# Score blocks of 32 keys written to their own partitions in a chunkwise scan

## The chip, the cores and the metric

The kernel runs on one core of a Trainium2 chip. The metric is the device time of one execution in microseconds (us); lower is better. All inputs and outputs are float32.

## The reference, cut to what matters

One layer of a diffusion trunk: an adaLN-modulated RMSNorm, an HGRN2 gated linear recurrence in both directions over 256 context and 2048 latent tokens with 8 heads of 128 channels, a projection, and then a gated ConvFFN. The change touches the recurrence alone. Per head and direction it is computed in chunks:

```python
b = jnp.cumsum(logf, axis=3)
b_ref = b[:, :, :, CHUNK // 2:CHUNK // 2 + 1]
b_last = b[:, :, :, -1:]
qe = q * jnp.exp(b - b_ref)
ke = k * jnp.exp(b_ref - b)
scores = jnp.einsum('bhnik,bhnjk->bhnij', qe, ke)
...
scores = jnp.where(mask, scores, 0.0)          # key not later than query
o_intra = jnp.einsum('bhnij,bhnjv->bhniv', scores, v)
kv = jnp.einsum('bhnjk,bhnjv->bhnkv', k * jnp.exp(b_last - b), v)
# state: s = decay * s + kv, chunk after chunk
o_inter = jnp.einsum('bhnik,bhnkv->bhniv', q * jnp.exp(b), s_start)
o = o_intra + o_inter
```

The result of the two directions is added, so for a pair of tokens there is one score: from the forward direction where the key is not later than the query, from the backward direction where it is not earlier (both on the diagonal).

## The kernel before, in words

The kernel has a mixer stage (the scan, up to about 1327 us of the profile), an output projection and a ConvFFN. Only the scan is changed. It walks over two groups of token tiles (`GROUPS`, line 39), in each over 8 heads, and in each over units of three tiles of 128 tokens (`unit`, line 362). For a unit, TensorE computes the gates of both directions, q and the values by products split into three passes (`mm3`, line 353; lines 356 to 358 are the bulk of its work). VectorE then makes cumulative products inside segments of 32 tokens (`S`, `F`, twelve segments in a unit), the keys `ke` and queries `qp` scaled within a segment, and from them by further factors `kd`, `qe`, `qi`, `qm`, `km` (`scaled`, line 489). `rt` holds the reciprocal of a segment's whole decay, `TB` and `TX` hold products of the segments' decays, made on GpSimd.

The steps of a tile are two closures. `part_a` (line 538) transposes `kd`, forms the tile's scores, merges them under masks into a 128 x 128 matrix `at` (keys on partitions, queries in columns). `part_b` (line 569) forms the state's update `kv`, the output `o` from the state and from `at`, and sends the results to a stash in DRAM. The closures of one unit are not run at once: `unit` returns them in an `order` list, and the next unit runs them between its own products (`fill`, `tick`), so that TensorE always has the big products to go on with. A scheduler below the program may move an instruction within its engine's queue.

The scores of a tile before: four products of 128 keys by 128 queries into one PSUM tile `sc` (lines 550, 551, 556, 557), of which each only fills a part that is used. `sc[:, 0]` and `sc[:, 1]` hold the forward and backward scores inside segments of 32 (with `qe`), `sc[:, 2]` those between the two segments of a 64-token pair (with the key copies `kx`), and `sc[:, 3]` those between the two pairs (`km`, `qm`). ScalarE copies two 64 x 64 corners of `sc[:, 3]` into the buffer `af` (lines 561 and 562), VectorE copies the rest under three masks (lines 563 to 565) and adds the two buffers (line 566).

A float32 product appears in the trace as two passes, each with its weight load (LDWEIGHTS) and its MATMUL. The program's one other place with products of fewer output rows than 128 within the scan is `ada_rest` (line 628): sums over partitions with a weight of one column.

Of the kernel before, what the change touches and what calls it, by code (L numbers as in the profile page):

```python
# [9 lines left out]
F32 = mybir.dt.float32  # L10
F32R = mybir.dt.float32r
BF16 = mybir.dt.bfloat16
U32 = mybir.dt.uint32
AF = mybir.ActivationFunctionType
OP = mybir.AluOpType
# [29 lines left out]
NS = 12  # L45
# [3 lines left out]
def body(ctx, tc, a, out):  # L49
    nc = tc.nc  # L50
    pe, act, dve, pool, sp = nc.tensor, nc.scalar, nc.vector, nc.gpsimd, nc.sync
# [38 lines left out]
    def pool_(stack, name, bufs=1, **kw):  # L90
        return stack.enter_context(tc.tile_pool(name=name, bufs=bufs, reuse_waits="tile", **kw))
# [94 lines left out]
    with ExitStack() as c0:  # L186
# [15 lines left out]
        first = [t for u in GROUPS[0] for t in u]  # L202
        for k in range(KT):
            for i in range(2):
# [3 lines left out]
                for n in range(2):  # L208
                    pe.matmul(mps[2 * i + n], silv[:, k, :], wt[:, n * 512:(n + 1) * 512],
                              start=k == 0, stop=k == KT - 1)  # L210
# [16 lines left out]
        for g in range(2):  # L227
            ks = slice(g * 4, g * 4 + 4)
            for j, hm in enumerate(hms):
                m = 0 if first[j] >= 0 else 1  # L230
# [9 lines left out]
        mx = p0.tile([128, 16], F32, name="mx")  # L240
# [38 lines left out]
    def mixer_scan():  # L279
        gp = pool_(c1, "gp", side="right")  # L280
        xp = pool_(c1, "xp", side="right")
        ps = pool_(c1, "ps", space=PSUM)
# [3 lines left out]
        def in_block(m, blk):  # L286
            n = 128 // blk
            pool.affine_select(out=m, in_=m, pattern=[[-blk, n], [0, blk]],
                               compare_op=OP.is_ge, fill=0.0, base=0, channel_multiplier=1)
            pool.affine_select(out=m, in_=m, pattern=[[blk, n], [0, blk]],  # L290
                               compare_op=OP.is_ge, fill=0.0, base=blk - 1, channel_multiplier=-1)

        def mask(name):
            m = fix.tile([128, 4, 32], F32, name=name)
            pool.memset(m, 1.0)
            return m

        mf, mb, mx = mask("mf"), mask("mb"), mask("mx")
        in_block(mb, 32)
        in_block(mx.rearrange("p (a c) b -> p a (c b)", c=2), 64)  # L300
        dve.tensor_tensor(mx, mx, mb, OP.subtract)
        in_block(mf, 32)
        for m, s in ((mf, 1), (mb, -1)):

            pool.affine_select(out=m, in_=m, pattern=[[32 * s, 4], [s, 32]],
                               compare_op=OP.is_ge, fill=0.0, base=0, channel_multiplier=-s)
        mfu, mbu, mxu = [m.rearrange("p a b -> p (a b)").bitcast(U32) for m in (mf, mb, mx)]
        d1 = fix.tile([128, NS, SEG], BF16, name="d1")
        pool.memset(d1, 0.0)
        pool.memset(d1[:, :, 0:1], 1.0)  # L310
# [11 lines left out]
        count = {"F": 0, "A": 0}  # L322
# [39 lines left out]
        def unit(h, w, u, tiles, todo, fine=False):  # L362
# [5 lines left out]
            g0 = 4 * s0  # L368
            lat = slice(g0, NS)
# [28 lines left out]
            for d in range(2):  # L398
# [4 lines left out]
                j = (1 - d) * NH + h  # L403
# [23 lines left out]
            q = gp.tile([128, nq], F32, name="q", tag="q", bufs=2)  # L427
# [24 lines left out]
            ke = gp.tile([128, 2, NS, 32], F32, name="ke", tag="ke", bufs=2)  # L452
# [9 lines left out]
            rt = gp.tile([128, 2, NS], F32, name="rt", tag="rt", bufs=2)  # L462
            dve.reciprocal(rt[:, :, lat], S[:, :, lat, 32])

            qp = gp.tile([128, 2, NS, 32], F32, name="qp", tag="qp", bufs=2)
# [23 lines left out]
            def scaled(dst, src, w):  # L489

                w = w[..., None].to_broadcast(list(w.shape) + [32])
                dve.tensor_tensor(dst, src, w, OP.mult)
# [7 lines left out]
            scaled(kd, ke, TBf[:, 0:4:3])  # L500


            qe = gp.tile([128, 2, NS, 32], F32, name="qe", tag="qe", bufs=2)
            scaled(qe[:, :, lat], qp[:, :, lat], rt[:, :, lat])
            qi = gp.tile([128, 2, NS, 32], F32, name="qi", tag="qi", bufs=2)
            scaled(qi[:, :, lat], qp[:, :, lat], TBf[:, 1:3, lat])

# [1 line left out]
            qm = gp.tile([128, NSC, 4, 32], F32, name="qm", tag="qm", bufs=2)  # L509
            km = gp.tile([128, NSC, 4, 32], F32, name="km", tag="km", bufs=2)  # L510
# [2 lines left out]
            scaled(km[:, s0:, 0:2], seg(ke[:, 1])[:, :, 0:2], TX[:, 1, s0:, 0:2])  # L513
            scaled(km[:, s0:, 2:4], seg(ke[:, 0])[:, :, 2:4], TX[:, 1, s0:, 2:4])

            kx = gp.tile([128, NS, 32], F32, name="kx", tag="kx", bufs=2)
            act.activation(kx[:, g0::2], ke[:, 1, g0::2], AF.Copy)
            act.activation(kx[:, g0 + 1::2], ke[:, 0, g0 + 1::2], AF.Copy)

            if s0:  # L520
                z = ps.tile([128, s0, 128], F32, name="z", tag="pj", bufs=3)
# [16 lines left out]
            def part_a(s):  # L538
                g4 = slice(4 * s, 4 * s + 4)
                tr = ps.tile([128, 2, 128], F32, name="tr", tag="tr")  # L540
                for d in range(2):
                    pe.transpose(tr[:, d], kd[:, d, g4], ident)
                kt = gp.tile([128, 2, 128], F32, name="kt", tag="kt", bufs=3)
                act.activation(kt, tr, AF.Copy)
                kts[s] = kt
                if s < s0:
                    return

                sc = ps.tile([128, 4, 128], F32, name="sc", tag="sc", bufs=2)
                pe.matmul(sc[:, 0], ke[:, 0, g4], qe[:, 0, g4], start=True, stop=True)  # L550
                pe.matmul(sc[:, 1], ke[:, 1, g4], qe[:, 1, g4], start=True, stop=True)

                c0 = qp[:, 0, 4 * s]
                qx = bass.AP(tensor=c0.tensor, offset=c0.offset,
                             ap=[list(c0.ap[0]), [64, 2], [(NS + 1) * 32, 2], [1, 32]])
                pe.matmul(sc[:, 2], kx[:, g4], qx, start=True, stop=True)
                pe.matmul(sc[:, 3], km[:, s], qm[:, s], start=True, stop=True)
                at = gp.tile([128, 128], F32, name="at", tag="at", bufs=2)
                af, ab = ABs[count["A"] % 2]
                count["A"] += 1  # L560
                act.activation(af[0:64, 64:128], sc[0:64, 3, 64:128], AF.Copy)
                act.activation(af[64:128, 0:64], sc[64:128, 3, 0:64], AF.Copy)
                dve.copy_predicated(af, mxu, sc[:, 2])
                dve.copy_predicated(af, mbu, sc[:, 0])
                dve.copy_predicated(ab, mfu, sc[:, 1])
                dve.tensor_tensor(at, af, ab, OP.add)
                ats[s] = at

            def part_b(s):
# [33 lines left out]
                sp.dma_start(stash[t][:, 0, h, 1], qi[:, 0, g4].rearrange("p g t -> p (g t)"))  # L603

            order = ((part_a, 0), (part_a, 1), (part_b, 0), (part_a, 2), (part_b, 1), (part_b, 2))
            return [lambda f=f, s=s: f(s) for f, s in order]

# [47 lines left out]
        for g, units in enumerate(GROUPS):  # L655
            for h in range(NH):
                if g == h == 0:
                    w = head0
                else:
                    w = load_feat(h)  # L660
                    load_vg(h, w)
                for u, tiles in enumerate(units):
                    todo, fine = list(unit(h, w, u, tiles, todo, fine)), False
                    if h > 0 and steps < 16 * (g + 1):
                        next(rest, None)
                        steps += 1
                    if g == h == u == 0:
                        todo, fine = with_h(todo, [m[-2:] for m in third], [None] * 3), True
                        todo = [m[0] for m in third[1:]] + todo
                    if g == 0 and h == NH - 2 and u == 2:  # L670
                        todo += [m[0] for m in new[0:2]]
                    if g == 0 and h == NH - 1:
                        loads = [m[0] for m in new[3 * u + 2:3 * u + 5]]
                        todo = with_h(todo, [m[1:] for m in new[3 * u:3 * u + 3]],
                                      loads + [None] * (3 - len(loads)))
                        fine = True
                    if g == 1 and h == NH - 1:
                        if u == 0:
                            todo.append(gate1)
                        for j, k in enumerate(range(3 * u, min(3 * u + 3, KT))):  # L680
                            todo.insert(len(todo) if u < 2 else j,
                                        lambda k=k: out_weight(k))
        for f in todo:
            f()

    mixer_scan()
    c1.close()

# [63 lines left out]
    qp = pool_(fq, "qp", side="right")  # L752
# [70 lines left out]
    first = [Pair(1, q) for q in range(2)]  # L823
# [225 lines left out]
    ps = pool_(fp, "psa", 2, space=PSUM)  # L1049
# [200 lines left out]
    ps = pool_(fb, "psb", 8, space=PSUM)  # L1250
# [169 lines left out]
    for s in range(N):  # L1420
        ph, c = divmod(s, NC)
# [84 lines left out]
```

## Time and profile before

| | us |
|---|---|
| median of 3 runs | 2856.59 (2854.42 to 2858.09) |
| span of the profiled execution | 2852.8 |
| TensorE (PE) busy in it | 2803.9 |
| its weight loads (PEld) | 2503.4 |
| VectorE (DVE) busy | 2080.8 |
| ScalarE (ACT) busy | 1176.5 |
| GpSimd (POOL) busy | 570.1 |

The span runs from the first to the last instruction of the profiled execution; the median of the runs is 3.8 us above it. Groups of instructions are shown as: line, engine, operation, output<-inputs, shapes, count | busy us in total, mean ns of one | idle time of the engine before them and what ended it. Rows of the timeline start with the start in us and the duration in us, and end with the number of instructions merged. In rows of one line's instructions the three numbers are the smallest, median and longest duration in ns, and 128*32 would mean 128 rows and 32 columns of the TensorE array. Matmuls overlap and their ends are modelled, so the distance of their starts is what they cost.

### The profile page before, as it was taken

Reading aid. Unit: us, or ns where it says so; the run is one execution under the profiler, and the core shown is the slowest. Engines: PE = TensorE matmul, PEld = TensorE weight load, DVE = VectorE, ACT = ScalarE, POOL = GpSimd, SP = SyncE. Lnnn points to the kernel's source line nnn. Section 1 sums busy time; section 2 is a strip of 40 time slices with the busy share of each in tenths; the row PEclk is TensorE's granted clock in tenths of the full one; section 3 lists DMA queues with packets and bytes.
Section 4 is the critical chain, followed back from the end, with each engine's and each line's share of the span. In section 5 each row is a group of like instructions: output and inputs, shape, how many; then the busy total and the mean of one; then the engine's idle time right before and its main releaser. Section 6 shows DMA issues by size and latency. Waiting matters only on the chain. (4 is left out here: it accounts for less than half of the span.)

```text
span 2852.8 us, 43739 instructions
## 1 busy us (share of the span) xinstructions
PE 2803.9 (98%) x16016; PEld 2503.4 (88%) x16016; DVE 2080.8 (73%) x3698; ACT 1176.5 (41%) x2517; POOL 570.1 (20%) x1020
## 2 busy tenths in 40 slices
PE   7999999999999999998999899999999999999999
PEld 4999999999999999998888688888888888887887
DVE  5766666677667566587898787777887777676887
ACT  5433333355333323333555444444444444333343
POOL 2111111121111111111111243433443342000001
PEclk9999999999999999999999999999999999999999
DMA  6222222222232222135778622225522223987663
GB/s 237 67 79 79 84 76 84 79 78 89 85 90 66 80 78 85 61 98 185 266 293 315 227 86 71 88 82 190 187 89 89 76 73 115 310 301 252 194 200 122
DMA packets 202623, 385.51 MB, mean 135 GB/s; under 512 B 26660, under 2 KB 117796, under 8 KB 197160
## 3 DMA queue, kind: packets, MB, share of 16 engines
q1 hardware_dynamic: 199672, 374.46, 39.1%
q10 hardware_dynamic: 2736, 8.26, 0.8%
q8 instruction: 126, 2.06, 0.3%
q14 instruction: 89, 0.73, 0.1%
HBM read 280.65 MB, written 101.99 MB: 134 GB/s over the span
## 5 line engine op out<-in xcount | busy, mean ns | idle before, releaser
L356 PE MATMUL z<-vh,hh 128*128 128x256 f32 (+1 forms) x1024 | 300.3, 293 | 0.0
L358 PE MATMUL z<-vh,hl 128*128 128x256 f32 (+1 forms) x1024 | 293.4, 287 | 0.0
L357 PE MATMUL z<-vl,hh 128*128 128x256 f32 (+1 forms) x1024 | 293.3, 286 | 0.0
L356 PE MATMUL z<-hh,wh 128*128 128x384 f32 x768 | 264.1, 344 | 0.7 <-ACT hh L80 0.7
L357 PE MATMUL z<-hl,wh 128*128 128x384 f32 x768 | 258.4, 336 | 0.5 <-DVE hl L81 0.5
L358 PE MATMUL z<-hh,wl 128*128 128x384 f32 x768 | 258.7, 337 | 0.0
L1338 PE MATMUL y<-wd,ml 128*128 128x512 f32 x600 | 234.0, 390 | 2.1 <-DVE ml L81 2.1
L1336 PE MATMUL y<-wd,mh 128*128 128x512 f32 x600 | 233.8, 390 | 0.9 <-DVE P L1390 0.7
L1337 PE MATMUL y<-wd,mh 128*128 128x512 f32 x600 | 233.5, 389 | 0.0
L356 PEld LDWEIGHTS z<-vh,hh 128*128 128x128 f32 x1024 | 196.3, 192 | 0.0
L357 PEld LDWEIGHTS z<-vl,hh 128*128 128x128 f32 x1024 | 196.1, 191 | 0.0
L358 PEld LDWEIGHTS z<-vh,hl 128*128 128x128 f32 x1024 | 195.8, 191 | 0.0
L81 DVE TENSOR_TENSOR w<-raw,w 128x512 fp32r<-128x512 f32 x180 | 141.9, 793 | 43.1 <-ACT w L80 41.1
L484 POOL COPY TX<-S 128x3 f32<-128x3 f32 x48 | 14.6, 304 | 792.4 <-DVE S L448 792.4
L80 ACT ACTIVATE w<-raw 128x512 fp32r<-128x512 f32 x180 | 111.8, 629 | 141.2 <-PE zd L741 78.6
L81 DVE TENSOR_TENSOR w<-s,w 128x512 fp32r<-128x512 f32 x126 | 122.3, 976 | 49.4 <-ACT w L80 48.6
L424 DVE TENSOR_TENSOR st<-z,st 128x128 f32<-128x128 f32 x127 | 36.5, 287 | 158.7 <-ACT st L423 158.6
L356 PEld LDWEIGHTS z<-hh,wh 128*128 128x128 f32 x768 | 145.3, 189 | 4.4 <-DVE acc L620 1.7
L419 ACT ACTIVATE v<-z 128x128 f32<-128x128 f32 x128 | 35.4, 277 | 271.1 <-PE z L358 271.1
L357 PEld LDWEIGHTS z<-hl,wh 128*128 128x128 f32 x768 | 145.2, 189 | 0.7 <-DVE hl L81 0.7
L358 PEld LDWEIGHTS z<-hh,wl 128*128 128x128 f32 x768 | 144.7, 188 | 0.0
L738 PE MATMUL zc<-rT,w 128*128 128x512 f32 x352 | 137.1, 389 | 2.7 <-ACT w L80 2.7
(337 smaller groups left out, 8119.8 us busy)
## 6 DMA issues: line engine op xcount, KB each, us to landing
raw<-in_w_up_dram SPq DMA_DIRECT2D x88, 512.0 KB, 3.8
raw<-in_w_in_dram SPq DMA_DIRECT2D x80, 512.0 KB, 3.7
lr<-m SPq DMA_DIRECT2D x49, 512.0 KB, 5.5
m<-r SPq DMA_DIRECT2D x66, 256.0 KB, 4.3
raw<-in_w_ada_dram SPq DMA_DIRECT2D x32, 512.0 KB, 4.5
stash<-st SPq DMA_DIRECT2D x125, 128.0 KB, 1.9
kq<-stash SPq DMA_DIRECT2D x15, 1024.0 KB, 7.4
og<-stash SPq DMA_DIRECT2D x15, 1024.0 KB, 6.3
```

The costliest lines, as they stand in the source:

```text
L80: act.activation(h, src, AF.Copy)
L81: dve.tensor_tensor(l, src, h.bitcast(F32), OP.subtract)
L356: pe.matmul(o, sh[:, k], mh[:, k], start=k == 0, stop=False)
L357: pe.matmul(o, sh[:, k], ml[:, k], start=False, stop=False)
L358: pe.matmul(o, sl[:, k], mh[:, k], start=False, stop=k == KT - 1)
L419: act.activation(v[:, s], z[:, 0:128], AF.Copy)
L424: dve.tensor_tensor(st[:, 1], z[:, 128:256], st[:, 1], OP.mult)
L484: pool.tensor_copy(TX[:, 0, :, 0], tot[:, 0, :, 1])
L738: pe.matmul(o, w[:, 0, k], r[:, :, 0, k], start=start and k == 0, stop=False, skip_group_check=True)
L1336: pe.matmul(z, lh, rh, start=start, stop=False, skip_group_check=True)
L1337: pe.matmul(z, lh, rl, start=False, stop=False, skip_group_check=True)
L1338: pe.matmul(z, ll, rh, start=False, stop=stop, skip_group_check=True)
```

## The change

Scores are formed in blocks of 32 keys, each written to the 32 partitions of its own keys: twelve products a tile, eight of them with 64 query columns and four with 32. The factor that carries a pair of 32-token segments over its inner border is multiplied in place, once, into the first or second segment's queries and keys (`halves`), so the scores of a whole 64-token pair of one direction come from one scaling; `qe` and `kx` go. The two PSUM tiles `scs` are made once, set to zero, and taken in turn, since blocks that no product writes are read under the mask. The masks now cover pairs of 64; the scores between the two pairs are written beside the forward ones in `sc[:, 0]` and come along with its masked copy, so the two copies on ScalarE and one masked copy on VectorE go.

```diff
-        mf, mb, mx = mask("mf"), mask("mb"), mask("mx")
-        in_block(mb, 32)
-        in_block(mx.rearrange("p (a c) b -> p a (c b)", c=2), 64)
-        dve.tensor_tensor(mx, mx, mb, OP.subtract)
-        in_block(mf, 32)
+        mf, mb = mask("mf"), mask("mb")
+        for m in (mf, mb):
+            in_block(m.rearrange("p (a c) b -> p a (c b)", c=2), 64)
         for m, s in ((mf, 1), (mb, -1)):
             pool.affine_select(out=m, in_=m, pattern=[[32 * s, 4], [s, 32]],
                                compare_op=OP.is_ge, fill=0.0, base=0, channel_multiplier=-s)
-        mfu, mbu, mxu = [m.rearrange("p a b -> p (a b)").bitcast(U32) for m in (mf, mb, mx)]
+        for i in range(2):
+            pool.memset(mb[64 * i:64 * i + 64, 2 - 2 * i:4 - 2 * i], 1.0)
+        mfu, mbu = [m.rearrange("p a b -> p (a b)").bitcast(U32) for m in (mf, mb)]
+        scs = [ps.tile([128, 2, 128], F32, name=f"sc{i}", tag=f"sc{i}", bufs=1) for i in range(2)]
+        for sc in scs:
+            dve.memset(sc, 0.0)
...
-            qe = gp.tile([128, 2, NS, 32], F32, name="qe", tag="qe", bufs=2)
-            scaled(qe[:, :, lat], qp[:, :, lat], rt[:, :, lat])
...
-            kx = gp.tile([128, NS, 32], F32, name="kx", tag="kx", bufs=2)
-            act.activation(kx[:, g0::2], ke[:, 1, g0::2], AF.Copy)
-            act.activation(kx[:, g0 + 1::2], ke[:, 0, g0 + 1::2], AF.Copy)
+            def halves(x, first):
+                c = x[:, 0, g0 + first]
+                step, inner = (32, [1, 32]) if len(x.shape) > 3 else (1, [0, 32])
+                return bass.AP(tensor=c.tensor, offset=c.offset,
+                               ap=[list(c.ap[0]), [(NS + 1 - 2 * first) * step, 2],
+                                   [2 * step, (NS - g0) // 2], inner])
+
+            for x, first in ((qp, 1), (ke, 0)):
+                dve.tensor_tensor(halves(x, first), halves(x, first), halves(rt, first), OP.mult)
...
-                sc = ps.tile([128, 4, 128], F32, name="sc", tag="sc", bufs=2)
-                pe.matmul(sc[:, 0], ke[:, 0, g4], qe[:, 0, g4], start=True, stop=True)
-                pe.matmul(sc[:, 1], ke[:, 1, g4], qe[:, 1, g4], start=True, stop=True)
-
-                c0 = qp[:, 0, 4 * s]
-                qx = bass.AP(tensor=c0.tensor, offset=c0.offset,
-                             ap=[list(c0.ap[0]), [64, 2], [(NS + 1) * 32, 2], [1, 32]])
-                pe.matmul(sc[:, 2], kx[:, g4], qx, start=True, stop=True)
-                pe.matmul(sc[:, 3], km[:, s], qm[:, s], start=True, stop=True)
+                sc = scs[count["A"] % 2]
+
+                def score(d, k, kc, q, qc):
+                    pe.matmul(sc[32 * kc.start:32 * kc.stop, d, 32 * qc.start:32 * qc.stop],
+                              k, q, start=True, stop=True, skip_group_check=True)
+
+                for j in range(4):
+                    kc, qc = slice(j, j + 1), slice(2 - j // 2 * 2, 4 - j // 2 * 2)
+                    score(0, km[:, s, kc], kc, qm[:, s, qc], qc)
+                for d in range(2):
+                    for j in range(4):
+                        kc = slice(j, j + 1)
+                        qc = slice(j // 2 * 2, j // 2 * 2 + 2) if j % 2 == 1 - d else kc
+                        score(d, ke[:, d, 4 * s + j], kc,
+                              qp[:, d, 4 * s + qc.start:4 * s + qc.stop], qc)
                 at = gp.tile([128, 128], F32, name="at", tag="at", bufs=2)
                 af, ab = ABs[count["A"] % 2]
                 count["A"] += 1
-                act.activation(af[0:64, 64:128], sc[0:64, 3, 64:128], AF.Copy)
-                act.activation(af[64:128, 0:64], sc[64:128, 3, 0:64], AF.Copy)
-                dve.copy_predicated(af, mxu, sc[:, 2])
                 dve.copy_predicated(af, mbu, sc[:, 0])
                 dve.copy_predicated(ab, mfu, sc[:, 1])
                 dve.tensor_tensor(at, af, ab, OP.add)
```

## The prediction

> **What bounds the kernel now.** I began with the page: the busy shares, and the strips in 40 slices.
>
> ```profile
> span 2852.8 us, 43739 instructions
> PE 2803.9 (98%) x16016; PEld 2503.4 (88%) x16016; DVE 2080.8 (73%) x3698; ACT 1176.5 (41%) x2517; POOL 570.1 (20%) x1020
> PE   7999999999999999998999899999999999999999
> PEclk9999999999999999999999999999999999999999
> ```
>
> TensorE is busy in nearly all slices, at the full granted clock; VectorE has a quarter of the span free and ScalarE more than half. An average of this kind does not settle one stage, so I asked next for the busy time in stretches of the scan, where all scores lie (their lines run from 86 to 1324 us), and for TensorE's own waits up to 1340 us.
>
> ```profile
> 300.00:700.00 400.00, 396.47 (x2809) 388.72 (x2808) 272.05 (x626) 169.54 (x478) 69.94 (x198) 1.00 0.27 84
> 700.00:1000.00 300.00, 300.00 (x2176) 297.08 (x2176) 195.88 (x434) 99.50 (x307) 38.74 (x126) 1.00 0.26 80
> ```
>
> ```profile
> PE kv L574 <- DVE Sf L593: 2.9, 5, 0.7
> ...
> PE sc L550 <- DVE AB L565: 0.3, 1, 0.3
> ```
>
> In the columns (stretch, then busy time of PE, its weight loads, DVE, ACT, POOL) PE is busy for 300.00 of 300.00 us while DVE is busy for 195.88 and ACT for 99.50. The longest wait of PE for DVE inside the scan sums to 2.9 us; that of the scores is 0.3 us. So in the scan time is TensorE time: what the change adds to PE's stream is paid in full, and what it takes from DVE and ACT is paid back only in those few waits.
>
> **What the change takes from DVE and ACT.** These are the groups it removes (a line, busy total, mean ns):
>
> ```profile
> L492 DVE TENSOR_TENSOR qe<-qp,rt 128x768 f32<-128x768 f32 (+1 forms) x48 | 41.3, 860 | 0.0
> L563 DVE COPY_PREDICATED AB<-mx,sc 128x128 f32<-128x128 uint32 x128 | 36.8, 290 | 2.3 <-ACT AB L562 2.3
> L562 ACT ACTIVATE AB<-sc 64x64 f32<-64x64 f32 x128 | 28.1, 220 | 2.6 <-issue 0.2
> L561 ACT ACTIVATE AB<-sc 64x64 f32<-64x64 f32 x128 | 27.5, 215 | 32.6 <-PE sc L557 32.5
> L517 ACT ACTIVATE kx<-ke 128x192 f32<-128x192 f32 (+1 forms) x48 | 16.6, 346 | 70.6 <-DVE ke L454 70.6
> L518 ACT ACTIVATE kx<-ke 128x192 f32<-128x192 f32 (+1 forms) x48 | 16.4, 342 | 53.9 <-DVE ke L453 53.8
> L453 DVE TENSOR_TENSOR ke<-S 128x384 f32<-128x384 f32 x48 | 26.8, 559 | 0.3
> ```
>
> ACT loses 28.1 + 27.5 + 16.6 + 16.4 = 88.6 us. DVE loses 41.3 + 36.8 = 78.1 us and gains two multiplications per unit of at most 384 columns, half of them from qp and half from ke; by the row of ke (L453, as many columns, 0.559 us) that is 48 × 2 × 0.559 = 54 us, so DVE ends 24 us lighter. All of it lies beside a busy PE. I put its worth at nothing, between 0 and the 3.2 us of the two waits above, which it could shorten; the set-up (two memsets of PSUM, other masks) runs once, on engines that PE does not wait for there, and I put it at nothing too.
>
> The new multiplications stand at the end of DVE's preparation of a unit, and the scores wait for them. Their cover is this stretch, where DVE ends a unit's last product (qm) and PE reaches that unit's first transposes:
>
> ```profile
> 708.59 0.35 DVE L492 TENSOR_TENSOR qm<-qp,TX 128x192 f32<-128x192 f32 x1
> ...
> 718.32 0.38 PE L542 MATMUL tr<-ident,kd 128*128 128x128 f32 x2
> ```
>
> That is 718.32 − 708.94 = 9.4 us of slack for 1.1 us of work, while qe's 0.9 us ahead of it goes. Queued behind it on DVE are the st products of the same unit, which read PE's z buffers and so free them, three in turn; they come 1.1 − 0.9 = 0.2 us later.
>
> **What it does to TensorE: the streaming.** Before, a tile has four score products, and each is two passes (256 instructions for 128 tiles):
>
> ```profile
> L550 PE MATMUL sc<-qe,ke 128*128 128x128 f32 x256 | 49.6, 275 | 0.3 <-DVE AB L565 0.3
> L556 PE MATMUL sc<-qp,kx 128*128 128x128 f32 x256 | 49.5, 275 | 0.0
> ```
>
> The mean of 275 ns is latency, since matmuls overlap. The cost is the distance between starts, read from the timeline (start, duration, line; two passes each):
>
> ```profile
> 702.83 0.39 PE L550 MATMUL sc<-qe,ke 128*128 128x128 f32 x2
> 703.06 0.39 PE L551 MATMUL sc<-qe,ke 128*128 128x128 f32 x2
> 703.28 0.39 PE L556 MATMUL sc<-qp,kx 128*128 128x128 f32 x2
> 703.50 0.39 PE L557 MATMUL sc<-qm,km 128*128 128x128 f32 x2
> 703.73 0.61 PE L574 MATMUL kv<-v,kt 128*128 128x128 f32 x4
> ```
>
> From 702.83 to 703.73 is 0.90 us for eight passes, 0.111 us a pass of 128 columns, and 0.89 us a tile. After, a tile has twelve products of 32 keys: eight with 64 query columns and four with 32. That is 16 passes of 64 and 8 of 32 columns, 1280 columns streamed in place of 1024, in 24 passes in place of 8.
>
> What such a short pass costs is not in this trace; three bounds are. If passes go in file at the same rate per column, it is 16 × 0.0555 + 8 × 0.0278 = 1.11 us a tile. If the four groups of 32 output partitions work side by side without loss, it is a quarter, 0.28 us. The upper bound is the shortest matmuls of this trace, sixteen transposes with two moving columns at the start:
>
> ```profile
> 34.98 0.90 PE L220 MATMUL mt<-ident,m 2*128 2x2 f32 x12
> ...
> L220 PE MATMUL mt<-ident,m x16: 195/196/218, 35.0 to 36.7; 2*128 2x2 f32 x16
> ```
>
> Twelve of them start over 0.90 − 0.196 = 0.70 us, 0.064 us from one weight load and matmul to the next though almost nothing streams; 24 of those are 1.54 us. I take a value between: the two passes of one call add into the same partitions and go in file, and a call into other partitions starts while the last pass of the call before still streams, half of that 0.064 us behind it. A call is then one pass and a start: 0.0555 + 0.032 = 0.088 us with 64 columns, 0.028 + 0.032 = 0.060 us with 32. The tile is 8 × 0.088 + 4 × 0.060 = 0.94 us, 0.05 us more than now, or 6 us over 128 tiles. It is nearest to the file (1.11 us), whose rate is the only one seen in a stream of products.
>
> The Trainium skill (TensorEngine Tiling (Array Packing), Instruction Overhead) speaks against cutting a dimension that is already small: a matmul has about 60 cycles of overhead, so one column takes as long as sixty. The 0.064 us of L220 says the same and more. By the page's figure at 2.4 GHz, 25 ns a pass, the 24 passes could not take under an estimated 0.60 us, and with 0.60 us for the 0.94 us above the sum below would come out near 2860 us.
>
> **The switch of the array.** The new products use 32 of the array's columns, everything around them 128. This trace shows what such a change costs at one place, the sums with a weight of one column (L628), between products of 128:
>
> ```profile
> 319.64 0.28 PE L357 MATMUL z<-vl,hh 128*128 128x256 f32 x1
> 319.76 0.28 PE L358 MATMUL z<-vh,hl 128*128 128x256 f32 x1
> 319.97 1.88 PE L628 MATMUL z<-acc,ones 128*1 128x512 f32 x4
> 321.77 0.44 PE L356 MATMUL z<-hh,wh 128*128 128x384 f32 x1
> 322.06 0.34 PE L357 MATMUL z<-hl,wh 128*128 128x384 f32 x1
> 322.23 0.34 PE L358 MATMUL z<-hh,wl 128*128 128x384 f32 x1
> ```
>
> ```profile
> L628 PEld LDWEIGHTS z<-acc,ones x16: 79/82/83, 320.0 to 1179.6; 128*1 128x1 f32 x16
> L628 PE MATMUL z<-acc,ones x16: 590/592/593, 320.0 to 1180.0; 128*1 128x512 f32 x16
> ...
> L550 PEld LDWEIGHTS sc<-qe,ke x256: 186/190/192, 86.4 to 1323.3; 128*128 128x128 f32 x128
> ```
>
> Going in: L358 follows L357 by 0.12 us, but L628 follows L358 by 0.21, so 0.09 us is lost. Going out: the four passes of L628 start (1.88 − 0.59) / 3 = 0.43 us apart, so the last ends its stream at 319.97 + 4 × 0.43 = 321.69. The following product should start there. The one after it starts at 322.06, and at the usual distance of 0.17 us (322.23 − 322.06) the first really started at 321.89: 0.20 us lost, as if the array ran empty and then waited for a whole weight load. Together 0.29 us for each excursion. A first load of 32 columns instead of one adds by the two load rows (190 − 82) / 127 × 31 = 26 ns. So 0.32 us a tile, 41 us in all, if every tile makes one excursion; in this timeline the scores of a tile stand together, between transposes and the kv products. It is zero if what L628 shows belongs to its own operands, and twice that if the order puts other products between a tile's twelve.
>
> **The sum.** 128 × (0.94 − 0.89 + 0.32) = 47 us on the profiled span of 2852.8 us, that is 2900 us; the median of the runs lies 3.8 us above that span, so 2904 us. About 0.2% (6 us) is what a measurement of this kernel can tell from no change.
>
> **The rivals.**
>
> *The groups really work side by side (faster).* With the switches at 0.32 us, the change gains as soon as a tile's 24 passes take less than 0.89 − 0.32 = 0.57 us. Full overlap, 0.28 us, gives 128 × (0.28 + 0.32 − 0.89) = −37 us, 2819 us; midway between 0.57 and 0.28, 0.43 us, it is 2838 us. For it: the blocks go to different partitions, and PE already lays weight loads beside matmuls. Against it: L220's 0.064 us, nearly nine times the 0.28 / 24 = 0.012 us that full overlap needs. The Trainium skill (TensorE: Matmul & The Clock Gate, Part 3) has column tiles running at once and reports 2.38 times the speed for three of them at 512 columns. By that figure the file's 1.11 us would be an estimated 0.47 us and the kernel some 13 us faster; no run here shows such short passes.
>
> *In file.* 1.11 us a tile: 128 × (1.11 + 0.32 − 0.89) = 69 us, 2926 us. For it: in the rows above no matmul starts closer to the one before than that one streams.
>
> *A floor for each load and matmul.* 24 × 0.064 = 1.54 us: 128 × (1.54 + 0.32 − 0.89) = 124 us, 2981 us. For it: L220. Against: its weights have 128 columns, these 32.
>
> *A wait in place of the removed copies.* If the in-place multiplications come so late that each unit's first scores wait out their 1.1 us, 48 × 1.1 = 53 us come on top of the sum, 2957 us. The slack of 9.4 us speaks against it.
>
> *The switches are not there, or cancel.* Without them 0.94 us gives 2863 us and 0.89 us gives no change.
>
> **How the numbers follow.** The forecast case has 0.37, in file 0.21, the floor 0.14, the late multiplications 0.05. Side by side has 0.17, all of it counted as faster; no switches or a cancellation within 0.2% has 0.06, of which 0.05 count as the same. Faster 0.17, same 0.05, slower 0.78. The range of 2838 to 2982 us takes in the floor and the weaker half of side by side.
>
> **What would show it.** In the changed profile the score line should have 3072 matmuls in place of 1024, its passes in other partitions some 0.03 us behind each other, and the distance from the last transpose to the first score and from the last score to the next product should be 0.1 and 0.2 us longer than the streams. DVE should be about 24 us and ACT about 89 us lighter, with PE as full as now and no new wait of PE for DVE. I am wrong if a tile's scores, switches included, take under 0.89 us, or if PE waits for ke or qp.

## The result and the profile after

The changed kernel takes 2822.8 us (median of 4 runs, 2821.26 to 2823.78) against 2856.2 us before: ratio 0.9882, 95% interval 0.9868 to 0.9896, or 33 us faster. I had forecast 2904 us and slower.

The page of the changed kernel (busy time and share of each engine, then the strips):

```profile
span 2821.9 us, 47353 instructions
PE 2771.7 (98%) x18064; PEld 2443.6 (87%) x18064; DVE 2061.7 (73%) x3619; ACT 1092.2 (39%) x2165; POOL 616.0 (22%) x1019
PE   8999999999999999998999899999999999999998
PEclk9999999999999999999999999999999999999999
```

TensorE has 2048 matmuls more (18064 against 16016, as expected: 3072 passes for 1024) and yet 32 us less busy time; it bounds the kernel as before. DVE is 19 us lighter and ACT 84 us, where 24 and 89 were forecast.

The groups of the scores and of the two new multiplications in the changed kernel:

```profile
L560 PE MATMUL sc<-qp,ke 128*32 128x32 f32 (+1 forms) x2048 | 47.0, 207 | 0.0
L560 PE MATMUL sc<-qm,km 128*32 128x64 f32 x1024 | 41.6, 231 | 0.0
L526 DVE TENSOR_TENSOR qp<-qp,rt 128x384 f32<-128x384 f32 (+1 forms) x47 | 24.0, 510 | 0.2
L526 DVE TENSOR_TENSOR ke<-ke,rt 128x384 f32<-128x384 f32 (+1 forms) x47 | 23.9, 508 | 0.0
```

The means of 207 and 231 ns again tell nothing of the cost. The timeline of one tile does, from the transposes ahead of the scores to the products behind them:

```profile
703.18 0.38 PE L550 MATMUL tr<-ident,kd 128*128 128x128 f32 x2
703.49 0.32 PE L560 MATMUL sc<-qm,km 128*32 128x64 f32 x8
703.63 0.36 PE L560 MATMUL sc<-qp,ke 128*32 128x32 f32 x16
703.91 0.44 PE L359 MATMUL z<-hh,wh 128*128 128x384 f32 x1
704.20 0.33 PE L360 MATMUL z<-hl,wh 128*128 128x384 f32 x1
704.37 0.33 PE L361 MATMUL z<-hh,wl 128*128 128x384 f32 x1
```

All 24 passes start between 703.49 and about 703.80 (the last row of scores ends at 703.99, and one pass of 32 columns lasts some 0.19 us), 0.31 us in all, 0.013 us a pass. The first product after them is recorded at 703.91; L361 follows L360 by 0.17 us, so by the start of L360 it really began at 704.03. From 703.18 to 704.03 is 0.85 us. Before, the same stretch began with these transposes:

```profile
702.62 0.38 PE L542 MATMUL tr<-ident,kd 128*128 128x128 f32 x2
```

From there to the kv product at 703.73 it took 1.11 us. The difference of 0.26 us over 128 tiles is 33 us.

### The profile page after: what moved, and what is told of

Its sections match the earlier page's. It is cut to its first block, busy times and chain, and to the rows that moved or that the text cites. A ratio compares the mean times of both kernels' runs of the same rounds, so it can differ in the third digit from the quotient of the medians.

```text
span 2821.9 us, 47353 instructions
## 1 busy us (share of the span) xinstructions
PE 2771.7 (98%) x18064; PEld 2443.6 (87%) x18064; DVE 2061.7 (73%) x3619; ACT 1092.2 (39%) x2165; POOL 616.0 (22%) x1019
## 5 line engine op out<-in xcount | busy, mean ns | idle before, releaser
L361 PE MATMUL z<-vh,hl 128*128 128x256 f32 (+1 forms) x1024 | 293.2, 286 | 0.0
L360 PE MATMUL z<-vl,hh 128*128 128x256 f32 (+1 forms) x1024 | 293.0, 286 | 0.0
L360 PE MATMUL z<-hl,wh 128*128 128x384 f32 x768 | 258.1, 336 | 0.5 <-DVE hl L81 0.5
L361 PE MATMUL z<-hh,wl 128*128 128x384 f32 x768 | 258.2, 336 | 0.0
L360 PEld LDWEIGHTS z<-vl,hh 128*128 128x128 f32 x1024 | 195.8, 191 | 0.0
L487 POOL COPY TX<-S 128x3 f32<-128x3 f32 x48 | 31.1, 648 | 753.7 <-DVE S L451 753.7
L361 PEld LDWEIGHTS z<-vh,hl 128*128 128x128 f32 x1024 | 195.5, 191 | 0.0
L360 PEld LDWEIGHTS z<-hl,wh 128*128 128x128 f32 x768 | 145.2, 189 | 0.8 <-DVE hl L81 0.7
L361 PEld LDWEIGHTS z<-hh,wl 128*128 128x128 f32 x768 | 144.8, 189 | 0.0
```

The lines of the kernel that those rows point to most:

```text
L360: pe.matmul(o, sh[:, k], ml[:, k], start=False, stop=False)
L361: pe.matmul(o, sl[:, k], mh[:, k], start=False, stop=k == KT - 1)
L487: pool.tensor_copy(TX[:, 0, :, 0], tot[:, 0, :, 1])
```

## Where the time came from, by stage

The scan's end can be dated by the first product of the stage behind it (`oi`), here in the kernel before, once more in a second profile of it, and in the changed kernel:

```profile
1327.12 1.95 PE L858 MATMUL oi<-Sb,kq 128*128 128x128 f32 x16
```

```profile
1326.91 1.95 PE L858 MATMUL oi<-Sb,kq 128*128 128x128 f32 x16
```

```profile
1290.42 1.95 PE L869 MATMUL oi<-Sb,kq 128*128 128x128 f32 x16
```

The scan is 36.7 us shorter. In these profiles the stages behind it are some 5 us longer, and a second profile of the kernel before was taken for this. 

> The kernel before, profiled once more. In its first profile the scan ends at 1327.1 us and the rest takes 1525.7 us; in the changed kernel's profile it is 1290.4 and 1531.5 us. If the rest differs from execution to execution, it is near 1531 us here; if the change costs something behind the scan, it is near 1526 us again.

The second profile of the kernel before has a span of 2853.9 us, so the rest takes 1527.0 us in it and 1525.7 in the first, against 1531.5 in the changed kernel; in the other kernels below it is 1529.2 to 1533.8 us. Where the difference lies is seen in stretches at equal distance from the scan's end; the column to read is the granted clock, third from the right. First the kernel before, then its second profile, then the changed kernel:

```profile
1327.00:1367.00 40.00, 34.84 (x192) 28.62 (x192) 32.78 (x95) 10.14 (x20) 7.24 (x5) 1.00 0.67 243
...
2535.00:2555.00 20.00, 19.77 (x88) 16.04 (x87) 18.48 (x23) 9.27 (x15) 0.00 (x0) 1.00 0.85 291
```

```profile
2535.00:2555.00 20.00, 16.64 (x66) 13.08 (x65) 18.79 (x23) 9.28 (x16) 0.00 (x0) 0.91 0.86 275
```

```profile
1290.00:1330.00 40.00, 34.80 (x186) 29.83 (x185) 31.30 (x90) 10.33 (x20) 7.21 (x5) 0.91 0.65 234
...
2505.00:2525.00 20.00, 17.86 (x71) 13.96 (x70) 18.74 (x23) 9.27 (x15) 0.00 (x0) 0.91 0.85 294
```

Right behind the scan the clock is full in both profiles of the kernel before and 0.91 in the changed kernel: 9% of 40 us, up to 3.6 us. The later dip of up to 1.8 us comes in one profile of the kernel before and not in the other. Together they are most of the 4.5 to 5.8 us. An obvious suspect is the order of PE's queue there: between two waits of PE the changed kernel has two products where the kernel before has twelve.

```profile
1332.48 1.58 PE L858 MATMUL oi<-Sb,kq 128*128 128x128 f32 x12 [3.42 <-DMA kq<-stash]
1335.62 0.33 PE L886 MATMUL tp<-ident,og 128*128 128x128 f32 x1 [1.57 <-DVE og L875]
```

```profile
1295.88 0.46 PE L869 MATMUL oi<-Sb,kq 128*128 128x128 f32 x2 [3.50 <-DVE rs L76]
1298.03 1.26 PE L897 MATMUL tp<-ident,og 128*128 128x128 f32 x4 [1.70 <-DVE og L886]
```

But the changed kernel with the removed copies put back (`copies_back`, below) has twelve again, behind a wait of 3.14 us, and its clock over the same 40 us is 0.91 all the same:

```profile
1297.04 2.40 PE L877 MATMUL oi<-Sb,kq 128*128 128x128 f32 x12 [3.14 <-DVE ss L889]
```

```profile
1292.00:1332.00 40.00, 35.86 (x183) 29.78 (x183) 31.83 (x91) 9.94 (x19) 7.21 (x5) 0.91 0.65 233
```

So the order does not explain the lower clock. Nor is it shown that the change causes it, for the clock of the kernel before differs from execution to execution too. In 19 later executions of it on one chip, the five with a mean granted clock of 0.996 have a mean span of 2854.0 us, the eight with 0.994 one of 2857.7 us. Its two profiles are at 0.997 and 0.996, and the eight executions of the changed kernel are all at 0.994 or 0.995. The 5 us may in part be a matter of which executions were profiled; the cause stays open. It touches neither the scan, where the clock is full in both kernels, nor the 36.7 us.

## The experiments

My theory after the result (A): products that write to different groups of 32 output partitions stream side by side in the array, so that a tile's 24 passes take 0.31 us instead of 0.89 us; switching the array to 32 columns and back costs about 0.31 us a tile on top; nothing else matters. The rivals: short passes are simply cheap wherever they are written (B); there is a floor for each load and matmul, unless the groups differ (C); the gain is the relief of DVE and ACT (D); the switches cost nothing. The kernels up to `copies_back` ran beside the kernel before at 2858.8 us; by the ratio of 0.9882 the changed kernel is at 2825 us there.

**All products into one group.** The output partitions of a product do not depend on its keys any more:

```diff
-                    pe.matmul(sc[32 * kc.start:32 * kc.stop, d, 32 * qc.start:32 * qc.stop],
+                    pe.matmul(sc[0:32, d, 32 * qc.start:32 * qc.stop],
```

> All twelve products of a tile are written to the same 32 output partitions; their number, sizes and order, and the switches of the array, stay. (The masks are set to zero, so the part of the output inside a chunk is left out.) Theory A, products in different groups of 32 output partitions stream side by side: now they must go in file, 16 x 0.0555 + 8 x 0.0278 = 1.11 us a tile in place of the 0.31 us of the changed kernel, 128 x 0.80 = 102 us more, about 2925 us. Rival B, a short pass is simply cheap (0.013 us) wherever it is written: no change, 2823 us. Rival C, a floor of 0.064 us for each load and matmul in one group: 1.54 us a tile, 2980 us.

Measured: 2921.9 us, ratio 1.0218 (1.0201 to 1.0235), 97 us above the changed kernel. Its timeline, one tile:

```profile
415.00 0.38 PE L552 MATMUL tr<-ident,kd 128*128 128x128 f32 x2
415.31 0.63 PE L562 MATMUL sc<-qm,km 128*32 128x64 f32 x8
415.78 0.86 PE L562 MATMUL sc<-qp,ke 128*32 128x32 f32 x16
416.57 0.45 PE L361 MATMUL z<-hh,wh 128*128 128x384 f32 x1
```

Eight passes of 64 columns take 415.78 − 415.31 = 0.47 us, 0.059 us each, and all 24 start within 416.64 − 0.19 − 415.31 = 1.14 us. That is the file of 1.11 us. B falls, and so does C: no floor of 0.064 us shows. The 0.064 us of the transposes at the start of the kernel was not a price of every load and matmul.

**Two groups.** The same with `g = 32 * (kc.start % 2)` and `sc[g:g + 32, ...]`.

> The products of a tile are written to two groups of 32 output partitions instead of four (masks zero as in the run with one group). Theory A: two streams side by side, 1.11 / 2 = 0.56 us a tile in place of 0.31, 128 x 0.25 = 32 us more, about 2855 us. Rival B: no change, 2823 us.

Measured: 2853.9 us, ratio 0.9981 (0.9972 to 0.9991), 29 us above the changed kernel.

```profile
699.18 0.42 PE L563 MATMUL sc<-qm,km 128*32 128x64 f32 x8
699.43 0.52 PE L563 MATMUL sc<-qp,ke 128*32 128x32 f32 x16
699.87 0.71 PE L588 MATMUL kv<-v,kt 128*128 128x128 f32 x4
```

The 24 passes start within 699.95 − 0.19 − 699.18 = 0.58 us. One, two and four groups take 1.14, 0.58 and 0.31 us: nearly in proportion, so the groups overlap almost without loss.

**Two excursions a tile.** The four products of `km` and `qm` moved ahead of the tile's transposes:

```diff
+                for j in range(4):
+                    kc, qc = slice(j, j + 1), slice(2 - j // 2 * 2, 4 - j // 2 * 2)
+                    score(0, km[:, s, kc], kc, qm[:, s, qc], qc)
                 tr = ps.tile([128, 2, 128], F32, name="tr", tag="tr")
...
-                for j in range(4):
-                    kc, qc = slice(j, j + 1), slice(2 - j // 2 * 2, 4 - j // 2 * 2)
-                    score(0, km[:, s, kc], kc, qm[:, s, qc], qc)
```

> The changed kernel with the four products between the pairs put ahead of the tile's two transposes, the other eight behind them, so that the array is switched to 32 columns and back twice a tile instead of once. Theory A, a switch empties the array (about 0.1 us in, 0.1 us plus an exposed weight load out; 0.15 us out into a transpose): about 0.27 us more a tile, 35 us, about 2858 us. Rival, switches cost nothing and what was seen at the one-column weights belongs to those: no change, 2823 us.

Measured: 2855.9 us, ratio 0.9992 (0.9983 to 1.0001), 31 us above the changed kernel.

```profile
700.18 0.34 PE L361 MATMUL z<-hh,vl 128*128 128x384 f32 x1
700.45 0.32 PE L552 MATMUL sc<-qm,km 128*32 128x64 f32 x8
700.70 0.44 PE L560 MATMUL tr<-ident,kd 128*128 128x128 f32 x2
701.07 0.38 PE L552 MATMUL sc<-qp,ke 128*32 128x32 f32 x16
701.38 0.49 PE L586 MATMUL kv<-v,kt 128*128 128x128 f32 x2
```

Both ways into the scores are there to see: 0.27 us from L361 to the first scores, where 0.17 us is usual, and 0.37 us from the recorded start of the transposes to the next scores, where two transposes take 0.22. One more excursion a tile, back by a transpose, costs 31 us / 128 = 0.24 us and gives back nearly the whole gain, though not one product was added.

**The removed copies put back.** The product `qe`, both key copies, both corner copies and one more masked copy a tile, added to the changed kernel:

```diff
+            qe = gp.tile([128, 2, NS, 32], F32, name="qe", tag="qe", bufs=2)
+            scaled(qe[:, :, lat], qp[:, :, lat], rt[:, :, lat])
...
+            kx = gp.tile([128, NS, 32], F32, name="kx", tag="kx", bufs=2)
+            act.activation(kx[:, g0::2], ke[:, 1, g0::2], AF.Copy)
+            act.activation(kx[:, g0 + 1::2], ke[:, 0, g0 + 1::2], AF.Copy)
...
+                act.activation(af[0:64, 64:128], sc[0:64, 0, 64:128], AF.Copy)
+                act.activation(af[64:128, 0:64], sc[64:128, 0, 0:64], AF.Copy)
+                dve.copy_predicated(af, mbu, sc[:, 0])
```

> The changed kernel with the removed work of VectorE and ScalarE put back beside the new: the product qe, the two key copies, the two corner copies and a second masked copy for every tile. Theory A, all of the gain is TensorE's: no change beyond some 3 us, 2823 to 2826 us. Rival D, the gain comes from the relief of VectorE and ScalarE: back to about 2856 us.

Measured: 2824.8 us, ratio 0.9882 (0.9868 to 0.9897), the ratio of the changed kernel.

```profile
span 2823.3 us, 47953 instructions
PE 2775.2 (98%) x18064; PEld 2445.5 (87%) x18064; DVE 2116.5 (75%) x3795; ACT 1170.1 (41%) x2517; POOL 586.0 (21%) x1019
```

DVE is 55 us and ACT 78 us busier than in the changed kernel, and the time does not move. D falls: what DVE and ACT are spared is worth nothing that these runs can tell.

The next four kernels ran together, beside the kernel before at 2859.6 us.

**The changed kernel again.** 

> The changed kernel itself, beside the next three on the same chip: 2823 us.

Measured: 2824.5 us, ratio 0.9877 (0.9863 to 0.9890).

**One scaling without blocks.** Three products of 128 by 128 for a tile instead of twelve:

```diff
+                sc = ps.tile([128, 3, 128], F32, name="sc", tag="sc", bufs=2)
+                pe.matmul(sc[:, 0], ke[:, 0, g4], qi[:, 0, g4], start=True, stop=True)
+                pe.matmul(sc[:, 1], ke[:, 1, g4], qi[:, 1, g4], start=True, stop=True)
+                pe.matmul(sc[:, 2], km[:, s], qm[:, s], start=True, stop=True)
...
+                dve.copy_predicated(af, mxu, sc[:, 2])
```

> The one scaling of pairs kept, but its scores formed by three products of 128 keys and 128 queries, with a third masked copy; no blocks of 32 columns, so no switch. (The queries of two of the products are replaced by others, qi, of the same shape, so the scores inside pairs are left out.) Theory A: 6 passes of 0.111 us, 0.67 us a tile against 0.89 before, 128 x 0.22 = 28 us less than before, about 2828 us. If the small blocks were the whole of the gain it would stay at 2856 us.

Measured: 2830.8 us, ratio 0.9900 (0.9886 to 0.9913), 6 us above the changed kernel and 29 us below the kernel before. In time, then, the larger part of the gain is that of dropping one full product. This kernel leaves the scores inside the pairs out, so no run shows the same time with all scores formed. The blocks of 32 stream in half the time of three full products (0.31 against 0.67 us), and the switches take nearly all of that back.

**One excursion a unit.** The products of all three tiles stand together, each tile with its own place in the two PSUM banks (two tiles in the first, written in the order 1, 0, 2); the transposes, masked copies and the rest stay where they were:

```diff
+        slots = [scs[0][:, 0], scs[0][:, 1], scs[1][:, 0]]
...
+            def products():
+                for s in (1, 0, 2):
+                    if s >= s0:
+                        tile_products(s, slots[s])
...
+                if s == 0:
+                    products()
```

> The changed kernel with the products of all three tiles of a unit put together behind the first transposes, so the array is switched once a unit instead of once a tile: 48 excursions in place of 128. Theory A: 80 x 0.31 = 25 us less, about 2798 us. Rival, switches cost nothing: 2823 us. Rival, the scores wait for a PSUM tile or the masked copies come too late: over 2823 us.

Measured: 2797.7 us, ratio 0.9782 (0.9769 to 0.9795).

```profile
715.16 0.38 PE L573 MATMUL tr<-ident,kd 128*128 128x128 f32 x2
715.47 0.32 PE L556 MATMUL sc<-qm,km 128*32 128x64 f32 x8
715.61 0.36 PE L556 MATMUL sc<-qp,ke 128*32 128x32 f32 x16
715.78 0.29 PE L556 MATMUL sc<-qm,km 128*32 128x64 f32 x8
715.90 0.36 PE L556 MATMUL sc<-qp,ke 128*32 128x32 f32 x16
716.07 0.29 PE L556 MATMUL sc<-qm,km 128*32 128x64 f32 x8
716.18 0.36 PE L556 MATMUL sc<-qp,ke 128*32 128x32 f32 x16
716.47 0.44 PE L361 MATMUL z<-hh,wh 128*128 128x384 f32 x1
```

Inside the excursion the next tile's passes go on at once (715.47, 715.78, 716.07): 0.31 and 0.29 us a tile. 2824.5 − 2797.7 = 27 us over 80 excursions saved is 0.33 us each.

**The same, ahead of the transposes.** `products()` stands before the transposes of the first tile instead of behind them.

> As the run with one excursion a unit, but the products stand ahead of the first transposes, so the array goes back to 128 columns with a transpose, whose weight load is shorter (0.056 us exposed in place of 0.107). Theory A: 48 x 0.05 = 2 us less than that run, about 2796 us; if the order of the queue is what matters, the two may differ by more.

Measured: 2795.4 us, ratio 0.9776 (0.9763 to 0.9790): 2 us less, as expected, but the two intervals overlap, so the 2 us are not shown. This version has the lowest median of all, 64 us below the kernel before.

## Why the prediction was wrong

The step that failed is the price of a short pass. I put a tile's 24 passes at 0.94 us; they take 0.31 us. In my working a product into other partitions starts only when the product before it is in its last pass; in fact the products of all four groups stream at once, for 0.31 us is close to a quarter of the file (0.28 us). Two readings led there.

First, I took 0.064 us, the distance of the transposes of L220, for an upper bound of one load and matmul and charged half of it as the distance of starts in different groups. With one group, 24 passes within 1.14 us and those of 64 columns at 0.059 us each show that the bound was not of that kind. L220 loads a weight of 128 columns for two streamed ones, and that load is probably what paced it; no run separates it. I also made too much of the 0.064 us: against the 0.012 us that full overlap needs it is some 5.5 times as much, not nearly nine.

Second, I named full overlap as a rival, 2819 us, and gave it, together with half overlap, 0.17, since it needs 0.012 us a pass. The measured pace is 0.013 us, and 2822.8 us is that rival's figure within 4 us. For such groups the Trainium skill (TensorE: Matmul & The Clock Gate, Part 3) has column tiles running at once, 2.38 times the speed for three; here four run 3.7 times (1.14 / 0.31) as fast as one, even with passes of 32 and 64 columns. The Trainium skill's other rule that I weighed, about 60 cycles of overhead for each matmul (TensorEngine Tiling (Array Packing), Instruction Overhead), did not hold across groups: 24 passes take half of the estimated 0.60 us.

The other steps, in their order:

- *TensorE bounds the scan, and DVE and ACT are worth nothing:* right, by the copies put back. PE's waits for DVE and ACT up to the scan's end, from the first scores on, sum to 6.4 us before and 6.6 us after, and the new multiplications (0.51 us each, forecast 0.56) delayed no score.
- *The switch, 0.32 us an excursion:* right. It shows as 703.49 − 703.29 = 0.20 us from the last transpose to the first score (0.11 usual), and 704.03 − 703.80 = 0.23 us from the last score to the real start of the next product, of which a pass of 32 columns takes 0.03. That is 0.09 + 0.20 = 0.29 us in this row; one excursion a unit instead of one a tile gives 0.33 us each, and the extra excursion back by a transpose 0.24 us. The sums of L628 with a one-column weight did foretell it.
- *The forecast of the cost in file, 1.11 us:* right for what it describes (1.14 us in one group). It was the wrong case.
- *Set-up and order of the queue:* right; the first score starts at about the same time (86.5 us before, 86.0 after), and a tile's twelve products stand together in the rows shown.
- *The sum:* with 0.31 in place of 0.94 us it is 128 × (0.31 − 0.89 + 0.32) = −33 us, where 33 were measured. So close a hit is in part luck: the scan alone became 36.7 us shorter, 3 to 4 us more than the sum, by nothing that these runs tell apart, and the stages behind it were longer in the changed kernel's profile.

What the signs at the prediction's end said: 3072 matmuls, the switches in and out and a full PE were there; the passes 0.03 us behind each other were not. The sign of being wrong was there too: a tile's scores, switches included, take 0.85 − 0.22 = 0.63 us, under the 0.89 us that I had named.

## What to carry to other kernels

Products with 32 output partitions each, written to the four different groups of partitions, ran side by side here: price a tile of them by the busiest group's streaming, not by the number of passes. Then count the excursions between products of 32 and of 128 columns, for each costs as much as a tile's whole set here (0.33 against 0.31 us). Gather small products before going back, as far as PSUM holds them; three tiles at a time gave 27 us here. And take a bound from a short instruction only after asking which of its parts, load or stream, set its pace.

## What the runs showed of the hardware that I had not expected

Four groups of output partitions overlap nearly perfectly even for passes of 32 and 64 columns with a weight load each: 1.14, 0.58 and 0.31 us for one, two and four groups. A switch to 32 columns and back costs 0.33 us an excursion (27 us over 80 of them); the extra excursions that go back by a transpose cost 0.24 us each (31 us over 128). And behind the scan, in stages whose code did not change, the granted clock over 40 us was 0.91 in the changed kernel and 1.00 in both profiles of the kernel before; the order of the queue does not explain it, and the cause stays open.
